# Products with ones in an encoder kernel: split high and low parts in place of float32

## The chip, the core and the metric

The kernel runs on one core of one Trainium2 chip. The core has a matrix engine (TensorE), a vector engine (VectorE), a scalar engine (ScalarE), a general engine (GpSimd), and a queue (SyncE) that starts most transfers. Each engine takes its instructions in order; they wait for one another through semaphores. On-chip memory has 128 partitions. Products are accumulated in eight banks of a memory of their own, 128 x 512 float32 each, which VectorE and ScalarE empty.

The metric is the device time of one execution in microseconds (us), as the median of several runs. A profile is one further execution, in which every instruction was recorded.

## The reference, cut to what matters

One layer of an encoder over a sequence of 1024 positions of width 1024, in float32, and a last norm:

```python
def _rmsnorm(x, w):
    return x * lax.rsqrt(jnp.mean(x * x, axis=-1, keepdims=True) + EPS) * w

h = _rmsnorm(x, attn_norm_w)
proj = h @ w_in                                  # 1024 x 8192
a = glu(first columns); a = dwconv31(a)          # 512 channels
mu = jnp.mean(a, axis=-1, keepdims=True)
var = jnp.mean(jnp.square(a - mu), axis=-1, keepdims=True)
a = silu((a - mu) * lax.rsqrt(var + EPS) * ln_w + ln_b) @ pw_w
b = (two gated scans of 8 heads, one per direction, normed and gated) @ hgrn_o_w
x = x + (sigmoid(g_a) * a + sigmoid(g_b) * b) @ w_out
h2 = _rmsnorm(x, ffn_norm_w)
gate, val = split(h2 @ ffn_w_up)                 # 2 x 2816 columns
x = x + (silu(dwconv3(gate)) * val) @ ffn_w_down
out = _rmsnorm(x, final_norm_w)
```

What matters here are the means: three of them (the first norm, the LayerNorm of the convolution, the norm ahead of the feed-forward part) run over a direction that the kernel keeps on the partitions.

## The kernel before, in words

**Layout and format.** Activations lie transposed: channels on the 128 partitions, positions along the free axis, in pages of 128 x 512 (a half of the sequence). A float32 operand of a large product is split into a high part, rounded to the format `float32r`, which TensorE takes at its full rate, and a low part, the rest (`split`, line 123: a ScalarE copy and a VectorE subtraction). A product is then three products of parts (`mm3`, lines 148 to 150). Where many columns share the activations, two by two blocks are multiplied with seven products in place of eight (`pair_job`, line 282), taken in the order 1, 2, 6, 7, 5, 4, 3. Pages `hx`, `hy` and `h` hold activation parts, `wp` and `wq` weight parts; in a pair job one `wq` page holds the weights of products 7 and 5, one holds those of 4.

**Order.** TensorE runs in program order. The other engines' instructions are put in order by a planner when the program is built: it takes what is ready first by the times that it assumes, and hands out the pages of a tag as they come free. `pin` (line 121) ties an instruction down: it may not be issued ahead of the one that was traced before it on its engine. A pinned instruction can wait for data, and then whatever stands behind it in the queue waits too. An instruction that is not pinned may be planned ahead of pinned ones.

**Streams.** The large products are a stream of pieces (`run_jobs`, line 194; a piece is two steps of three products, six in all). Between pieces runs a tick, which brings forward the split of a later job's weights (`Weights`, line 169) and the chores that are due (`later`, line 158). In the feed-forward part these splits are pinned.

**The norms.** The sum over partitions of a page of squares is taken by four narrow products, the page as weights against a column of ones (line 611); they leave the 512 sums on partitions, as 128 x 4. Root and power run there on GpSimd (`rstd_small`, line 590). To have the factor of each position on every partition, the four columns are written as four diagonals of a 128 x 512 page, and a float32 product of an all-ones matrix with it copies each diagonal over all partitions (`spread`, line 595, the product in line 601). The diagonals are made by four ScalarE operations (line 600), or, for the norm ahead of the feed-forward part, by one pinned GpSimd operation (line 621). The LayerNorm's mean is one float32 product of the all-ones matrix with the sum of four pages (line 1065).

**Where they stand.** The first half of x is normed before it is turned, and uses none of this. `second_norm` (line 752) norms the second half. The LayerNorm loop (line 1056) runs twice, between pieces of the pair jobs. The norms ahead of the feed-forward part (line 1759) run inside its first job: the factor is applied only to the results, so the products start without it. Piece 1 of that job is filled in line 1742; then line 1757 puts off the splits of the `hy` pages for product 4 by four and five ticks (one of them is of `t6`, which line 1726 makes in a page of tag `tm`); two more pieces follow, then the two norms up to their diagonals (line 1761), one piece, the fetches for product 3, seven pieces, and then the two products of line 601 and their copies (line 1766). The weights of products 7 and 5 of that job are split at the tick of its fourth piece, those of product 4 at its seventh.

**Pages.** Tag `tm` has four pages of 128 x 512, which temporary results of all parts share, the diagonals too.

**Stores.** As the residual sum x2 is made (`x2_evac`, line 1581), each of its 16 pages, scaled by the norm's weights, is stored to `d_h2` (line 1599). Line 1764 reads back four of them.

Of the kernel before, what the change touches and what calls it, by code (L numbers as in the profile page):

```python
# [18 lines left out]
P = 128  # L19
# [28 lines left out]
def tile_hybrid_encoder(  # L48
# [51 lines left out]
    def bank(tag):  # L100
        return ps.tile([P, H], F32, tag=tag, name=nm(tag), bufs=BANKS[tag])

    def page(pool, tag, bufs, dt=F32):
        return pool.tile([P, H], dt, tag=tag, name=nm(tag), bufs=bufs)

    def tmp():
        return page(mp, "tm", 4)
# [373 lines left out]
    make_identity(nc, ident)  # L481
    mhalf = cp.tile([P, 1], F32, name="mhalf")
    G.memset(mhalf, -0.5)
    ones_m = cp.tile([P, P], F32, name="ones_m")
    cp.tile([P, ALIGN // 4 - 8], F32, name="offset")
    G.memset(ones_m, 1.0)

# [63 lines left out]
    def scratch(name, *dims):  # L551
        if not dims:
            return dp.tile([P, H], F32, name=name)
        return [scratch(f"{name}_{i}", *dims[1:]) for i in range(dims[0])]
# [12 lines left out]
    d_x0 = dp.tile([P, 4, ND, P], F32, name="d_x0")  # L567
    d_xt = [[d_x0[:, :, k, :], scratch(f"d_xt_{k}")] for k in range(ND)]
    d_x2 = scratch("d_x2", ND, 2)
    d_h2 = scratch("d_h2", ND, 2)  # L570
    d_t4 = scratch("d_t4", ND // 2)
    d_g = scratch("d_g", NF, 2)
    d_us = [dp.tile([P, 4, ND // 2 * P], F32, name=f"d_us_{n}") for n in range(3)]
# [16 lines left out]
    def rstd_small(dst, ss, n, late=False):  # L590
        hold = pin if late else lambda i: i
        hold(G.tensor_scalar(dst, ss, 1.0 / n, EPS, op0=ALU.mult, op1=ALU.add))
        hold(G.tensor_tensor(dst, dst, mhalf.to_broadcast(list(dst.shape)), op=ALU.pow))

    def spread(r, b, rs, diag=None, late=False):

        if diag is None:
            diag = tmp()
            for c in range(4):
                A.activation(diag[:, c * P : (c + 1) * P], ident, AF.Copy, scale=r[:, c : c + 1])  # L600
        T.matmul(b, ones_m, diag, start=True, stop=True)
        do = A.copy(rs, b)
        if late:
            pin(do)
        return rs

    def rstd_over_partitions(sq, n, tag, rs, early=False):

        b = bank(tag)
        for c in range(4):  # L610
            T.matmul(
                b[:, c : c + 1], sq[:, c * P : (c + 1) * P], ones_m[:, 0:1], start=True, stop=True
            )
        r = cp.tile([P, 4], F32, name=nm("r4"), tag="r4", bufs=2)
        V.tensor_copy(r, b[:, 0:4])
        rstd_small(r, r, n, early)
        diag = None
        if early:
            diag = tmp()
            pin(  # L620
                G.tensor_tensor(
                    diag.rearrange("p (c e) -> p c e", c=4),
                    view(ident, 0, [[0, 4], [1, P]]),
                    view(r, 0, [[1, 4], [0, P]]),
                    op=ALU.mult,
                )
            )
        yield
        yield spread(r, bank(tag), rs, diag, early)

    def first_norm():

# [119 lines left out]
    def second_norm():  # L752
        xs, ss = x_in[4:], ss2
        banks = []

        def turn(k):
            b = bank("tr")
            for i in range(4):
                T.transpose(b[:, i * P : (i + 1) * P], xs[i][:, k * P : (k + 1) * P], ident)
            banks.append(b)  # L760

        turn(0)
        yield
        rstd_small(ss, ss, D)
        rs = spread(ss, bank("ob"), page(p0, "rs", 1))
        yield
        for k in range(ND):
            b = banks[k]
            raw, xt = ev(), tmp()
            V.scalar_tensor_tensor(raw, b, vec("attn", k), rs, op0=ALU.mult, op1=ALU.mult)  # L770
            hl = split(hx(), hx(), raw, G)
            A.copy(xt, b)
            if k + 1 < ND:
                turn(k + 1)
            nc.sync.dma_start(d_h[k][1], raw)
            nc.sync.dma_start(d_xt[k][1], xt)
            if k < NK2:
                h12.append(hl)
            else:
                ht[3].append(hl)  # L780
            yield
# [268 lines left out]
    def total(ts, o):  # L1050
        V.tensor_tensor(o, ts[0], ts[1], op=ALU.add)
        for t in ts[2:]:
            V.tensor_tensor(o, o, t, op=ALU.add)
        return o

    for half in range(2):
        xs = []
        for j in range(NCW):
            if j % 2 == 0:
                both = p1.tile([P, 2, H], F32, tag="ca", name=nm("cx"), bufs=2)  # L1060
            nc.sync.dma_start(both[:, j % 2, :], d_cv[j][half])
            xs.append(both[:, j % 2, :])
        s_pairs.fill(LN_FILL)
        mean = bank("ob")
        T.matmul(mean, ones_m, total(xs, tmp()), start=True, stop=True)
        for t in xs:
            V.scalar_tensor_tensor(t, mean, -1.0 / CW, t, op0=ALU.mult, op1=ALU.add)
        s_pairs.fill(LN_FILL)
        sqs = [tmp() for _ in xs]
        for sq, t in zip(sqs, xs):  # L1070
            A.activation(sq, t, AF.Square)
        rstd = rstd_over_partitions(total(sqs, sqs[0]), CW, "ob", tmp())
        next(rstd)
        s_pairs.fill(5)
        rs = next(rstd)
        for j, xn in enumerate(xs):
            V.tensor_tensor(xn, xn, rs, op=ALU.mult)
# [503 lines left out]
    def x2_evac(i):  # L1581


        def evac(half, acc):
            xt = ev()
            to = xt if half else xt.rearrange("p (c t) -> p c t", c=4)
            nc.sync.dma_start(to, d_xt[i][half])
            t = page(p4, "x2", 2)
            V.tensor_tensor(t, acc, xt, op=ALU.add)
            nc.sync.dma_start(d_x2[i][half], t)  # L1590
            if i == 0:
                A.activation(sq_sum[half], t, AF.Square)
            else:
                sq = tmp()
                A.activation(sq, t, AF.Square)
                V.tensor_tensor(sq_sum[half], sq_sum[half], sq, op=ALU.add)
            g = page(p4, "xq", 5)
            A.activation(g, t, AF.Copy, scale=vec("ffn", i))
            nc.sync.dma_start(d_h2[i][half], g)
            x2[i][half] = g  # L1600

        return evac
# [158 lines left out]
        next(st)  # L1761
    s_ffn.fill(1)
    for k in range(NK2):
        late_parts(5 + k // 2, 3, fetch(d_h2[k + NK2][1]))
    s_ffn.fill(7)
    rstd2 = [next(st) for st in stats]

# [301 lines left out]
```

## Time and profile before

| | |
|---|---|
| time, median of 3 runs | 1722.05 us (1721.24 to 1723.18) |
| span of the profiled execution, first to last instruction | 1720.0 us |
| ScalarE, line 600: 12 diagonal pieces | 0.39 us each |
| GpSimd, line 621: 2 diagonal pages | 1.04 and 1.69 us |
| stores of line 1599 | 16 of 256 KB, SyncE 0.33 us each, landed after 3.8 us |
| transfers, all | 308.28 MB, mean 179 GB/s |

The profile gives a span alone, from the first to the last instruction; the runs' times are those of the device. The median of the runs is 2.05 us above the profiled span. In its rows PE is TensorE, ACT is ScalarE, DVE is VectorE, POOL is GpSimd, SP is SyncE. A row names the line of the kernel, the operation, what it writes and reads, and in brackets how long the engine stood idle before it and for whom. Line 124 is the body of `split`, so its rows are told apart by the pages that they write. A TensorE record lasts longer than the distance to the next one, since products overlap; what a product takes of the stream is read from the distance of starts. A float32 product is two records.

### The profile page before, as it was taken

Reading aid. Unit: us, or ns where it says so; the run is one execution under the profiler, and the core shown is the slowest. Engines: PE = TensorE matmul, PEld = TensorE weight load, DVE = VectorE, ACT = ScalarE, POOL = GpSimd, SP = SyncE. Lnnn points to the kernel's source line nnn. Section 1 sums busy time; section 2 is a strip of 40 time slices with the busy share of each in tenths; the row PEclk is TensorE's granted clock in tenths of the full one; section 3 lists DMA queues with packets and bytes.
Section 4 is the critical chain, followed back from the end, with each engine's and each line's share of the span. In section 5 each row is a group of like instructions: output and inputs, shape, how many; then the busy total and the mean of one; then the engine's idle time right before and its main releaser. Section 6 shows DMA issues by size and latency. Waiting matters only on the chain.

```text
span 1720.0 us, 30762 instructions
## 1 busy us (share of the span) xinstructions
PE 1699.1 (99%) x11902; PEld 1416.2 (82%) x11902; DVE 1256.6 (73%) x1937; ACT 825.0 (48%) x1544; POOL 240.7 (14%) x281
## 2 busy tenths in 40 slices
PE   8999999999999999999999999999999999999998
PEld 6878888788788888888888888888888888888787
DVE  4599999745779888888656466667777776657865
ACT  6443443233577777776442245444434433542334
POOL 1212222200001111111100002122222222000110
PEclk9999999999999999999999999999999999999999
DMA  8777888854673444435689466577778776783842
GB/s 281 238 181 177 201 191 189 203 160 148 202 261 91 146 127 133 128 116 200 223 277 279 143 205 199 147 159 153 165 166 174 171 172 154 229 266 102 215 95 99
DMA packets 337096, 308.28 MB, mean 179 GB/s; under 512 B 17582, under 2 KB 249142, under 8 KB 336950
## 3 DMA queue, kind: packets, MB, share of 16 engines
q1 hardware_dynamic: 289590, 267.51, 49.1%
q0 software_dynamic: 47360, 38.81, 15.5%
q8 instruction: 93, 1.52, 0.4%
q14 instruction: 53, 0.43, 0.1%
HBM read 201.40 MB, written 87.03 MB: 168 GB/s over the span
## 4 chain that ended last, share of the span: by engine, by line
PE 61%; DVE 1%; ACT 1%; DMA 0%; issue 0%; POOLq 0%; ACTq 0%; SPq 0%; DVEq 0%
PE mm L148 14%; PE mm L150 14%; PE mm L149 14%; PE sc L148 3%; PE sc L150 3%; PE sc L149 3%; PE ob L1375 2%; PE tr L148 1%; PE tr L150 1%; PE tr L149 1%; PE sc L1197 1%; PE sc L1283 1%; PE mm L1334 1%; PE sc L1334 1%; PE ob L1197 0%
## 5 line engine op out<-in xcount | busy, mean ns | idle before, releaser
L148 PE MATMUL mm<-hx,wp 128*128 128x512 f32 x1068 | 426.9, 400 | 2.3 <-ACT tm L851 1.4
L150 PE MATMUL mm<-hx,wp 128*128 128x512 f32 x1068 | 416.9, 390 | 0.5 <-DVE wp L124 0.5
L149 PE MATMUL mm<-hx,wp 128*128 128x512 f32 x1068 | 416.2, 390 | 0.0
L124 ACT CAST wp<-wr 128x1024 fp32r<-128x1024 f32 (+2 forms) x147 | 147.3, 1003 | 217.8 <-PE mm L149 180.3
L148 PEld LDWEIGHTS mm<-hx,wp 128*128 128x128 f32 x1068 | 200.6, 188 | 45.0 <-DVE ev L800 2.2
L150 PEld LDWEIGHTS mm<-hx,wp 128*128 128x128 f32 x1068 | 200.5, 188 | 44.4 <-DVE wp L124 1.6
L149 PEld LDWEIGHTS mm<-hx,wp 128*128 128x128 f32 x1068 | 200.8, 188 | 39.2 <-issue 0.7
L124 DVE TENSOR_TENSOR wp<-wr,wp 128x1024 fp32r<-128x1024 f32 (+2 forms) x145 | 169.1, 1167 | 39.1 <-ACT wp L124 32.7
L1039 DVE SCALAR_TENSOR_TENSOR acc<-gl,v_b,acc 128x1024 f32<-128x1024 f32 x120 | 148.7, 1272 | 0.4
L440 ACT COPY su<-mm 128x512 f32<-128x512 f32 x82 | 47.7, 582 | 80.1 <-PE mm L150 80.1
L1315 POOL DMA_DIRECT2D S<-D x64 | 36.3, 573 | 284.2 <-ACT S L1313 155.6
L1144 DVE TENSOR_TENSOR qF<-qF,tb 128x512 f32<-128x512 f32 x96 | 65.5, 684 | 13.3 <-ACT A L1178 12.7
L124 ACT CAST wq<-sw 128x1024 fp32r<-128x1024 f32 x41 | 43.2, 1053 | 61.2 <-PE mm L149 32.9
L148 PE MATMUL tr<-hx,wp 128*128 128x512 f32 x180 | 70.5, 392 | 0.0
L150 PE MATMUL tr<-hx,wp 128*128 128x512 f32 x180 | 70.1, 389 | 0.0
L149 PE MATMUL tr<-hx,wp 128*128 128x512 f32 x180 | 70.0, 389 | 0.0
L1144 DVE TENSOR_TENSOR kG<-kG,tb 128x512 f32<-128x512 f32 x96 | 65.5, 685 | 4.7 <-ACT A L1178 2.5
L1652 DVE SCALAR_TENSOR_TENSOR tm<-gp,v_a,tm 128x512 f32<-128x512 f32 x88 | 66.0, 750 | 4.0 <-ACT tm L1650 2.0
L301 POOL DMA_DIRECT2D sw<-in_ffn_w_up_dram x38 | 49.8, 1498 | 116.5 <-DMA sw<-in_ffn_w_up_dram 76.7
L148 PE MATMUL mm<-hy,wp 128*128 128x512 f32 x164 | 64.2, 391 | 0.0
L148 PE MATMUL sc<-hy,wq 128*128 128x512 f32 x164 | 64.2, 391 | 0.0
L150 PE MATMUL sc<-hy,wq 128*128 128x512 f32 x164 | 63.8, 389 | 0.0
(375 smaller groups left out, 3723.3 us busy)
## 6 DMA issues: line engine op xcount, KB each, us to landing
wr<-in_w_in_dram SPq DMA_DIRECT2D x48, 512.0 KB, 5.0
wr<-in_ffn_w_up_dram SPq DMA_DIRECT2D x22, 512.0 KB, 5.1
sw<-in_w_in_dram SPq DMA_DIRECT2D x38, 256.0 KB
d_g<-ft SPq DMA_DIRECT2D x38, 256.0 KB, 2.0
sw<-in_ffn_w_up_dram SPq DMA_DIRECT2D x38, 256.0 KB, 3.5
sw<-in_ffn_w_up_dram POOLq DMA_DIRECT2D x38, 256.0 KB, 6.2
wr<-sw POOLq DMA_DIRECT2D x32, 256.0 KB, 3.3
wr<-wr POOLq DMA_DIRECT2D x32, 256.0 KB, 3.4
```

The lines of the kernel that those rows point to most:

```text
L124: parts = A.copy(hi, src), eng.tensor_tensor(lo, src, hi.bitcast(F32), op=ALU.subtract)
L148: T.matmul(acc, whi[:, k, :], ahi, start=first, stop=False, skip_group_check=again)
L149: T.matmul(acc, whi[:, k, :], alo, start=False, stop=False, skip_group_check=again)
L150: T.matmul(acc, wlo[:, k, :], ahi, start=False, stop=last, skip_group_check=again)
L301: G.dma_start(o, a, accum_op=ALU.add)
L440: A.copy(t, acc)
L1039: V.scalar_tensor_tensor(acc, g[:, k : k + S], tap(k), acc, op0=ALU.mult, op1=ALU.add)
L1144: return V.tensor_tensor(o, a, b, op=op)
L1315: G.dma_start(S_t[g : g + 32, :, g : g + 32], D_t[g : g + 32])
L1334: T.matmul(u[:, sl], kTs[d][:, sl], v[:, c, :], start=True, stop=True)
L1375: T.matmul(o[:, sl], l, r, start=(n == 0), stop=(n == len(terms) - 1))
L1652: V.scalar_tensor_tensor(c, g[:, o + k : o + k + H], vec("fdw", k * NF + j), c, op0=ALU.mult, op1=ALU.add,)
```

## The change

- The all-ones matrix is made as a `float32r` page `ones_r`; `ones_m` is a float32 view of it.
- `diagonals` takes the place of the ScalarE diagonals: the 128 x 4 factors are split into tiny high and low pages, and for each a page of diagonals is made by one VectorE multiplication with the identity. For the norms ahead of the feed-forward part (`early`) the high page stays on GpSimd, and all of these operations are pinned, the split too.
- `all_rows` multiplies the all-ones matrix with the high and the low page, in `float32r`, into the same bank. `spread` uses it, and the LayerNorm's mean, whose sum is split for it.
- In `second_norm` and in the LayerNorm root and diagonals are traced ahead of the pieces that come before the product.
- Of the stores to `d_h2` only the four that are read back are left.

```diff
-    ones_m = cp.tile([P, P], F32, name="ones_m")
+    ones_r = cp.tile([P, P], F32R, name="ones_r")
+    ones_m = ones_r.bitcast(F32)
...
-    d_h2 = scratch("d_h2", ND, 2)
+    d_h2 = scratch("d_h2", ND)
...
-    def spread(r, b, rs, diag=None, late=False):
-
-        if diag is None:
-            diag = tmp()
-            for c in range(4):
-                A.activation(diag[:, c * P : (c + 1) * P], ident, AF.Copy, scale=r[:, c : c + 1])
-        T.matmul(b, ones_m, diag, start=True, stop=True)
-        do = A.copy(rs, b)
+    def diagonals(r, early=False):
+
+        hold = pin if early else lambda i: i
+        tiny = [cp.tile([P, 4], F32R, name=nm("rp"), tag=tag, bufs=2) for tag in ("rh", "rl")]
+        split(*tiny, r, V, early)
+        pages = [page(mp, "tm", 4, F32R) for _ in range(2)]
+        for n, (d, t) in enumerate(zip(pages, tiny)):
+            eng = G if early and n == 0 else V
+            hold(
+                eng.tensor_tensor(
+                    d.rearrange("p (c e) -> p c e", c=4),
+                    view(ident, 0, [[0, 4], [1, P]]),
+                    view(t.bitcast(F32), 0, [[1, 4], [0, P]]),
+                    op=ALU.mult,
+                )
+            )
+        return pages
+
+    def all_rows(b, parts):
+        for n, part in enumerate(parts):
+            T.matmul(b, ones_r, part, start=n == 0, stop=n == len(parts) - 1)
+        return b
+
+    def spread(b, rs, diags, late=False):
+        do = A.copy(rs, all_rows(b, diags))
...
         rstd_small(r, r, n, early)
-        diag = None
-        if early:
-            diag = tmp()
-            pin(
-                G.tensor_tensor(
...
-                )
-            )
+        diags = diagonals(r, early)
         yield
-        yield spread(r, bank(tag), rs, diag, early)
+        yield spread(bank(tag), rs, diags, early)
...
         turn(0)
+        rstd_small(ss, ss, D)
+        diags = diagonals(ss)
         yield
-        rstd_small(ss, ss, D)
-        rs = spread(ss, bank("ob"), page(p0, "rs", 1))
+        rs = spread(bank("ob"), page(p0, "rs", 1), diags)
...
-        mean = bank("ob")
-        T.matmul(mean, ones_m, total(xs, tmp()), start=True, stop=True)
+        sums = [page(mp, "tm", 4, F32R) for _ in range(2)]
+        mean = all_rows(bank("ob"), split(*sums, total(xs, tmp()), V))
...
-            nc.sync.dma_start(d_h2[i][half], g)
+            if i >= NK2 and half:
+                nc.sync.dma_start(d_h2[i], g)
...
-        late_parts(5 + k // 2, 3, fetch(d_h2[k + NK2][1]))
+        late_parts(5 + k // 2, 3, fetch(d_h2[k + NK2]))
```

More of the change, by code (lines that the diff above doesn't have):

```diff
@@ L616, in rstd_over_partitions @@
         rstd_small(r, r, n, early)
-        diag = None
-        if early:
-            diag = tmp()
-            pin(
[L621 to L625, printed above, removed]
-                )
-            )
+        diags = diagonals(r, early)
         yield
-        yield spread(r, bank(tag), rs, diag, early)
+        yield spread(bank(tag), rs, diags, early)
     def first_norm():
```

## The prediction

> **What bounds the kernel now.** I read the page first: the busy shares, then the chain of work that ended last.
>
> ```profile
> span 1720.0 us, 30762 instructions
> ...
> PE 1699.1 (99%) x11902; PEld 1416.2 (82%) x11902; DVE 1256.6 (73%) x1937; ACT 825.0 (48%) x1544; POOL 240.7 (14%) x281
> ...
> PE 61%; DVE 1%; ACT 1%; DMA 0%; issue 0%; POOLq 0%; ACTq 0%; SPq 0%; DVEq 0%
> ```
>
> TensorE is busy for 99% of the span and holds nearly all of the chain that is attributed. So a product that gets cheaper shortens the kernel by its own price, an operation on another engine costs nothing while TensorE has its operands in time, and whatever makes TensorE wait is paid in full, since no idle time follows that could take it back. TensorE's order is written out by hand: a late operand stops everything behind it.
>
> Next the timeline of TensorE around one of the edited products (columns: start, duration, engine, line, operation), and the views of lines 601 and 1065.
>
> ```profile
> 422.51 0.40 PE L150 MATMUL mm<-hx,wp 128*128 128x512 f32 x1
> 422.74 1.02 PE L601 MATMUL ob<-tm,ones_m 128*128 128x512 f32 x2
> 423.20 0.80 PE L148 MATMUL mm<-hx,wp 128*128 128x512 f32 x1
> 423.84 0.40 PE L149 MATMUL mm<-hx,wp 128*128 128x512 f32 x1
> ...
> 426.11 0.39 PE L150 MATMUL mm<-hx,wp 128*128 128x512 f32 x1
> ```
> ```profile
> L601 PE MATMUL ob<-tm,ones_m x8: 590/592/595, 39.7 to 1073.6; 128*128 128x512 f32 x8
> ...
> L601 PE MATMUL sc<-tm,ones_m x2: 590/592/595, 1072.3 to 1072.7; 128*128 128x512 f32 x2
> ```
> ```profile
> L1065 PE MATMUL ob<-tm,ones_m x4: 590/592/595, 405.9 to 449.6; 128*128 128x512 f32 x4
> ```
>
> The starts of a steady stream lie 0.227 us apart (423.84 to 426.11 is ten products). From 422.51 to 423.84 there are two such steps, 0.454, and the float32 product: 1.33 - 0.454 = 0.876 us. Each float32 product is two records, so there are 5 of line 601 and 2 of line 1065, seven in all.
>
> **The change part by part.** *Seven products* of 0.876 us become seven pairs of full-rate products, 2 x 0.227 = 0.454 each: 0.42 us saved, seven times, **-2.9 us**. This lies on the path. The 16 narrow float32 products of line 611 stay.
>
> *The dropped stores* (12 of 16 of line 1599) were issued by SyncE beside TensorE's work; no wait of TensorE in that stage names a transfer: 0. If they slow the loads beside them, the gain is below what the waits show, so also 0.
>
> *Norms one and two* (the second half of x, and the LayerNorm twice). ScalarE loses four diagonal pieces each time; VectorE gains a tiny subtraction and two 512-wide multiplications, and each mean gains a ScalarE cast and a VectorE subtraction ahead of its product. The tightest of these is the second LayerNorm mean:
>
> ```profile
> 444.79 0.69 DVE L1053 TENSOR_TENSOR tm<-tm,cx 128x512 f32<-128x512 f32 x1
> ...
> 446.96 1.22 DVE L124 TENSOR_TENSOR wp<-wr,wp 128x1024 fp32r<-128x1024 f32 x1
> ...
> 449.44 0.69 DVE L800 TENSOR_TENSOR ev<-tr,su 128x512 f32<-128x512 f32 x1 [1.26 <-issue]
> ```
> ```profile
> 449.19 1.02 PE L1065 MATMUL ob<-tm,ones_m 128*128 128x512 f32 x2
> ```
>
> The sum is there at 445.48, the product starts at 449.19: 3.7 us of cover. A cast (0.62) and a subtraction (0.69) take 1.3; behind the subtraction already queued (to 448.18) the low part is there at 448.9. Hidden, so 0; should VectorE take the 0.69 and another 1.22 first, it costs about 2.
>
> *The two norms ahead of the feed-forward part* are where a wait is added. These are the rows of the kernel before: ScalarE, VectorE, GpSimd, then TensorE.
>
> ```profile
> 1060.84 0.58 ACT L440 COPY su<-mm 128x512 f32<-128x512 f32 x1
> 1061.32 1.05 ACT L124 CAST wq<-sw 128x1024 fp32r<-128x1024 f32 x1
> 1064.03 1.32 ACT L124 CAST hy<-ft 128x512 fp32r<-128x512 f32 x2 [1.66 <-DMA ft<-d_t]
> ...
> 1066.15 0.62 ACT L124 CAST hy<-ft 128x512 fp32r<-128x512 f32 x1
> ...
> 1067.20 0.62 ACT L124 CAST hy<-tm 128x512 fp32r<-128x512 f32 x1
> ```
> ```profile
> 1061.48 0.15 DVE L615 COPY r<-ob 128x4 f32<-128x4 f32 x1
> 1063.00 0.69 DVE L1680 TENSOR_TENSOR gp<-tr,su 128x512 f32<-128x512 f32 x1 [1.37 <-PE tr L150]
> 1063.61 1.38 DVE L124 TENSOR_TENSOR wq<-sw,wq 128x1024 fp32r<-128x1024 f32 x1
> 1064.91 1.28 DVE L124 TENSOR_TENSOR hy<-ft,hy 128x512 fp32r<-128x512 f32 x2
> ...
> 1068.05 0.68 DVE L124 TENSOR_TENSOR hy<-tm,hy 128x512 fp32r<-128x512 f32 x1
> ```
> ```profile
> 416.30 0.20 POOL L592 TENSOR_SCALAR r<-r 128x4 f32<-128x4 f32 x1 [59.11 <-DVE r L615]
> 416.58 1.03 POOL L593 TENSOR_TENSOR r<-r,mhalf 128x4 f32<-128x4 f32 x1
> ```
> ```profile
> 1062.62 1.29 POOL L1726 TENSOR_TENSOR tm<-tm,xq 128x512 f32<-128x512 f32 x1
> ...
> 1064.11 0.93 POOL L592 TENSOR_SCALAR r<-r 128x4 f32<-128x4 f32 x1
> 1065.13 1.33 POOL L593 TENSOR_TENSOR r<-r,mhalf 128x4 f32<-128x4 f32 x1
> 1066.54 1.04 POOL L621 TENSOR_TENSOR tm<-ident,r 128x512 f32<-128x512 f32 x1
> ...
> 1069.68 1.69 POOL L621 TENSOR_TENSOR tm<-ident,r 128x512 f32<-128x512 f32 x1
> ```
> ```profile
> 1065.47 0.39 PE L148 MATMUL sc<-h,wq 128*128 128x512 f32 x1
> 1065.70 0.39 PE L149 MATMUL sc<-h,wq 128*128 128x512 f32 x1
> 1065.92 0.39 PE L150 MATMUL sc<-h,wq 128*128 128x512 f32 x1
> ```
>
> Before, the norms put nothing but free copies on ScalarE and VectorE here; the whole chain of root and diagonal is GpSimd's, and it has until 1072. Now `split(*tiny, r, V, early)` puts a tiny ScalarE copy and a tiny VectorE subtraction into it for each norm, and `pin` ties them, and the low diagonals, into program order. A pinned instruction may not be issued ahead of the one traced before it on its engine. Counting the steps of the stream: the two norms are traced behind the third piece of the first feed-forward job, and the cast of `wq` (weights of products 7 and 5, 1061.32) at the tick of the fourth piece, pinned too. So that cast, which now runs while GpSimd works, **must stand behind both tiny copies**, and the second copy needs GpSimd's second root. Behind the cast stand the pinned `hy` casts, and on VectorE the low part of `wq` stands behind the second low diagonal. TensorE wants the high part of `wq` at 1065.47 and the low one at 1065.92.
>
> The chain, in the clock of before. GpSimd starts its first scale at 1064.11; VectorE is now idle beside it, so 0.20 and 1.03 as at 416: root at 65.4. Tiny copy: no row shows one on ScalarE; between VectorE's 0.15 and the 0.62 of a 512-wide cast, 0.2, near the copy of the same size: 65.65. First high diagonal on GpSimd 1.04 to 66.75; VectorE's low one waits its turn and holds GpSimd's next scale to 67.4 (the 0.93 at 1064.11 ends with VectorE's 1.38 at 1063.61: the two take turns). Root 68.5, second tiny copy 68.7, cast of `wq` to 69.75.
>
> Then the page that the second low diagonal needs. Tag tm has four pages. `t6` holds one until its `hy` cast and subtraction are done (rows hy<-tm); the first norm's two diagonals hold two until their products, which stand behind products 7 and 5; the second high diagonal, ready first, takes the last. So the second low diagonal waits for `t6`: the `hy` casts follow the `wq` cast, each some 0.53 behind the last, the fourth ends at 71.9, its subtraction (0.68) at 72.6. Those VectorE subtractions are pinned behind line 1680, not behind the diagonal, so nothing closes a circle. Low diagonal 0.69 to 73.35, low `wq` 1.22 to 74.6. TensorE's product of 65.92 starts at 74.6: **+8.7 us**. From below: if GpSimd's diagonal is the one that waits for `t6`, VectorE's goes at 68.9, low `wq` is done near 71: +5.1, and 4.7 with every step at its shortest. From above: two other subtractions (0.68 and 1.22) ahead of the diagonal: +10.6.
>
> *The clock.* TensorE then stands nearly still for 4 us, does two products, and stands again.
>
> ```profile
> 1712.00:1712.50 0.50, 0.16 (x2) 1.00 0.00 0
> ...
> 1714.50:1715.00 0.50, 0.00 (x0) 0.50 0.00 0
> ```
> ```profile
> 13.67 6.39 PE L894 MATMUL mm<-hx,wp 128*128 128x512 f32 x18
> ...
> 20.69 1.63 PE L894 MATMUL mm<-hx,wp 128*128 128x512 f32 x6
> ```
>
> At the end of the kernel the granted clock is halved some two us behind the last work. At the start, 18 products took 6.39 us, where at 0.227 a step and 0.39 for the last it would be 4.25: 2.1 lost to a slow start, part of it waits for operands. I take 1.7 for the return from such a stop, bounds 0 and 2.1. [...]
>
> **Sum**: -2.9 + 8.7 + 1.7 = +7.5. The profiled span of 1720.0 becomes 1727.5; the median of the runs is 2.05 above that span, and I carry this over: **1729.5**.
>
> **The rivals.**
> *The other page* (GpSimd's second diagonal waits for `t6`): -2.9 + 5.1 + 1.7 = +3.9, 1725.9; without the clock's part 1724.2. For it: only which of two instructions gets the last page. Against: VectorE's needs one step more (0.15) before it can start.
> *Cheaper products and no wait*, on the other side: if the cast and subtraction of `wq` stay done by 1065.47 and 1065.92, only -2.9 is left, 1719.1, within 0.2%. It is decided there: the second tiny copy would have to be done by 1064.2, 4.5 us sooner than I make it. For it: the ScalarE row at 1061.32 shows how early the cast can go when nothing holds it. Against: the pin, and GpSimd's 1062.62 row, behind which the roots start.
> *One more wait*: the LayerNorm mean's low part late as above, or the longer VectorE queue: +2 to +3 on the forecast, 1732. *Not what it says*: a full-rate product might cost what a float32 one does; then the seven pairs save nothing, and 2.9 more joins the forecast, 1732.4; against it stand the 0.227 steps of the same format.
>
> **How the numbers follow.** Forecast 0.58, other page 0.22, no wait 0.10, one more wait or no saving 0.10. About 0.2% (3.4 us) is what a measurement of this kernel can tell from no change. Slower: forecast and last rival, 0.68, and nearly half of the other page: 0.78. Same: the rest of the other page and most of the no-wait case, 0.19. Faster: 0.03, if small shifts elsewhere add to the saving. The range leaves out the no-wait case and the far end: 1723.5 (other page, short steps, no clock loss) to 1733.0 (+10.6 and 2.1: 1731.9, and a us of shifts).
>
> **What would show it.** Right: full-rate records on the edited lines, adding 0.454 to the stream; the cast wq<-sw behind two tiny copies near 1068.7; TensorE idle before its first sc<-h,wq, again at the third, which waits for VectorE; the second low diagonal behind hy<-tm; a clock below 1 for some us. Wrong: the cast at 1061 as before, or a tiny copy ready by 1064. The forecast falls if the roots start earlier, or if a later wait of TensorE shrinks by what this one adds.

## The result, and the profile after

The changed kernel takes 1732.78 us (median of 5 runs, 1732.18 to 1733.41). The kernel before takes 1723.17 (median of 5 runs, the three of the table above among them). The ratio is 1.0061, with a 95% interval of 1.0049 to 1.0074: slower by 8 to 13 us. The page of the kernel after:

```profile
span 1730.8 us, 30738 instructions
...
PE 1699.8 (98%) x11902; PEld 1416.6 (82%) x11902; DVE 1263.4 (73%) x1952; ACT 824.3 (48%) x1539; POOL 238.9 (14%) x281
```

The span grew by 10.8 us, TensorE's busy time by 0.7. So in sum the growth is time in which TensorE stands: in its busy time, products that last longer (below) and products that became cheaper about cancel. The view of the waits says for whom (waiting engine, what it writes and its line, whom it waited for, sum, times, longest):

```profile
PE sc L148 <- ACT wq L124: 4.0, 1, 4.0
PE sc L150 <- DVE wq L124: 4.0, 1, 4.0
PE mm L148 <- DVE ev L809: 2.6, 3, 1.3
```
```profile
PE mm L148 <- DVE ev L800: 0.7, 1, 0.7
```

The first two are new. The third stood at 0.7 before the change (the second view, of the kernel before, where the line was 800). The timelines of ScalarE, VectorE and TensorE show the first two in the making.

```profile
1065.52 0.19 ACT L124 CAST rp<-r 128x4 fp32r<-128x4 f32 x1 [4.01 <-POOL r L594]
1068.56 0.19 ACT L124 CAST rp<-r 128x4 fp32r<-128x4 f32 x1 [2.85 <-POOL r L594]
1068.66 1.04 ACT L124 CAST wq<-sw 128x1024 fp32r<-128x1024 f32 x1
...
1071.65 0.62 ACT L124 CAST hy<-tm 128x512 fp32r<-128x512 f32 x1
```
```profile
1072.39 0.68 DVE L124 TENSOR_TENSOR hy<-tm,hy 128x512 fp32r<-128x512 f32 x1
1073.11 0.69 DVE L605 TENSOR_TENSOR tm<-ident,rp 128x512 fp32r<-128x512 f32 x1
1073.72 1.22 DVE L124 TENSOR_TENSOR wq<-sw,wq 128x1024 fp32r<-128x1024 f32 x1
```
```profile
1065.33 0.39 PE L150 MATMUL mm<-hx,wp 128*128 128x512 f32 x1
1069.76 0.79 PE L148 MATMUL sc<-h,wq 128*128 128x512 f32 x1 [4.04 <-ACT wq L124]
1070.35 0.63 PE L149 MATMUL sc<-h,wq 128*128 128x512 f32 x1
1074.99 0.79 PE L150 MATMUL sc<-h,wq 128*128 128x512 f32 x1 [4.01 <-DVE wq L124]
1075.58 0.63 PE L148 MATMUL sc<-h,wq 128*128 128x512 f32 x1
1076.01 0.63 PE L149 MATMUL sc<-h,wq 128*128 128x512 f32 x1
...
1079.85 0.42 PE L149 MATMUL mm<-hx,wq 128*128 128x512 f32 x1
1080.11 0.39 PE L150 MATMUL mm<-hx,wq 128*128 128x512 f32 x1
```

ScalarE does two casts of 0.19 us, and in front of each it stands, 4.01 and 2.85 us, for GpSimd's root. The cast of the page `wq`, begun at 1061.32 before, comes behind them at 1068.66. On VectorE the second low diagonal waits for its page until `t6` is split (hy<-tm at 1072.39), and the low part of `wq` comes behind it. TensorE's third product starts at 1074.99, in place of 1065.92. Then its starts lie 0.43 us apart (1075.58 to 1076.01) where 0.227 is usual, until 1079.85. The granted clock by stretches (from and to; busy us and instructions of PE, PEld, DVE, ACT, POOL; clock; DMA share; GB/s):

```profile
1066.00:1070.00 4.00, 0.24 (x1) 0.24 (x2) 1.54 (x2) 1.44 (x3) 3.40 (x4) 0.95 0.40 153
1070.00:1080.00 10.00, 5.99 (x14) 4.20 (x15) 6.15 (x8) 4.08 (x8) 0.00 (x0) 0.51 0.40 117
1080.00:1085.00 5.00, 5.00 (x24) 4.05 (x23) 3.11 (x5) 2.88 (x7) 0.00 (x0) 1.00 0.10 29
```

For ten microseconds TensorE has half its clock.

**A ledger.** TensorE runs the same large products in the same order in both kernels, so the start of one product, after minus before, says how much has been lost up to there. Ahead of the feed-forward part, at 1059.6 us, it is +0.1. Each of the five other cheaper products shows its 0.4 us at its place, but waits have taken all of it back by then. The three waits for line 809, up to 343 us, take 1.8 us more than the waits at the same products before (0.70 and 0.09 us there), and one at 859 us takes 0.5 more (0.77 after, 0.24 before). Another -0.8 in that +0.1 is no work of the change: at 30 us, ahead of every edited product, the kernel after already stands at -0.8, since the clock rises to full at 14.92 us in its trace and at 17.72 in the trace before. At the third late product the ledger is +9.1; at the last one at half clock +11.4; behind the two cheaper feed-forward products +10.7; at the end +10.7. So the large loss stands in the feed-forward part, and behind 1085 us nothing is added and nothing taken back.

### The profile page after: what moved, and what is told of

The parts are those of the page before. It is cut to its first block, busy times and chain, and to the rows that moved or that the text cites. A ratio compares the mean times of both kernels' runs of the same rounds, so it can differ in the third digit from the quotient of the medians.

```text
span 1730.8 us, 30738 instructions
## 1 busy us (share of the span) xinstructions
PE 1699.8 (98%) x11902; PEld 1416.6 (82%) x11902; DVE 1263.4 (73%) x1952; ACT 824.3 (48%) x1539; POOL 238.9 (14%) x281
## 3 DMA queue, kind: packets, MB, share of 16 engines
q8 instruction: 93, 1.52, 0.4%
## 4 chain that ended last, share of the span: by engine, by line
PE 37%; issue 12%; DMA 1%; DVE 1%; ACT 0%; POOL 0%; SPq 0%; POOLq 0%; ACTq 0%; DVEq 0%
PE mm L150 8%; PE mm L148 8%; PE mm L149 8%; PE sc L150 3%; PE sc L148 3%; PE sc L149 3%; PE tr L149 1%; PE tr L148 1%; PE tr L150 1%; PE ob L1384 0%; DMA tm<-d_g 0%; DMA d_a<-ev 0%; DMA tm<-d_gc 0%; PE sc L1922 0%; DMA A<-d_bm 0%
```

## The experiments

Each run's ratio is to the kernel before, run on the same chip, with its 95% interval. I call "ledger" the comparison of starts just described.

**1. The feed-forward norms alone, undone and done.** Undone in the changed kernel:

```diff
-        diags = diagonals(r, early)
-        yield
-        yield spread(bank(tag), rs, diags, early)
+        if early:
+            diag = tmp()
+            pin(
+                G.tensor_tensor(
+                    diag.rearrange("p (c e) -> p c e", c=4),
+                    view(ident, 0, [[0, 4], [1, P]]),
+                    view(r, 0, [[1, 4], [0, P]]),
+                    op=ALU.mult,
+                )
+            )
+            yield
+            b = bank(tag)
+            T.matmul(b, ones_m, diag, start=True, stop=True)
+            pin(A.copy(rs, b))
+            yield rs
+            return
+        diags = diagonals(r)
+        yield
+        yield spread(bank(tag), rs, diags)
```

> The changed kernel, with the two norms of the FFN stage alone as they were before: one float32 diagonal by GpSimd, one float32 product each. Theory: the whole loss arises there. TensorE's first product after the FFN norms ran 10.6 us later than before, counted from the products just ahead of the stage, and nothing was added behind it, so the time falls by 10.6, to about 1722.2 us, level with the kernel before (ratio 0.999 to 1.001); the two waits of 4.0 us on the pages wq are gone, and the products behind them run at the full clock again. Rival: a good part of the loss is spread (the longer wait for the layer norm's mean, 0.9 us, a lower clock all over, later transfers): then it stays at 1725 us or above.

Measured: 1721.51 us, ratio 0.9997 (0.9988 to 1.0006). The loss is gone, and both waits on `wq` with it.

The other way round, the same edit alone put into the kernel before (`split` of the 128x4 factors, GpSimd's high and VectorE's low diagonal, two full-rate products, for the two feed-forward norms only):

> The kernel before, with the edit of the two FFN norms alone: the rest is as before. Theory: the edit of these two norms makes the whole difference and the other five cheaper products give nothing at the end, so 1723.2 + 10.6 = 1733.8 us (ratio 1.006). Rival: the five other products' saving of 5 x 0.42 = 2.1 us is contained in the changed kernel's time, which would then be 1734.9 us or more here; a second rival, that the loss needs the other edits too, gives less than 1731 us.

Measured: 1733.67 us, ratio 1.0066 (1.0051 to 1.0081), with the same two waits of 4.0 us. Both sides agree: this one place makes the loss. The interval of the first run leaves the worth of the five other products open between -2.1 and +1.0 us.

**2. What holds the page.** Two edits, each in a kernel of its own, that move one step of the order: in the first this one split isn't pinned, in the second `t6` comes from another ring of pages.

```diff
-                w[7], w[5] = both(col, pool)
+                w[7], w[5] = both(col, pool, late and not now)
...
-        t7, t6, t5 = tmp(), tmp(), tmp()
         last = k == NK2 - 1
+        t7, t6, t5 = tmp(), ev() if last else tmp(), tmp()
```

> The changed kernel; only the place of one split moves: the w7/w5 page of the FFN's first job isn't held behind the norms' instructions any more, so ScalarE can cast it between the norms' two tiny copies and VectorE makes its low part ahead of the second diagonal. Nothing else is changed. Theory: the stall is the order of instructions on ScalarE and VectorE, so it shrinks by what the page comes earlier: low part done at about 70 us in place of 75 (1000 us left out), the third product about 4 us late in place of 9, a time of 1726 to 1728 us. Rival: what holds the page is not the place in the order (its operands, or a buffer that comes free late): no change, 1732.8 us.

> The changed kernel; one of the three temporaries of the last pair in the FFN's stage ahead takes a page of another ring, so that the second norm's diagonals don't wait for it. Theory: VectorE's second diagonal no longer sits ahead of the page's low part until its page is free, the low part ends at about 71.3 us (1000 left out) in place of 75, and the stall falls by 3.4 to 3.9 us: about 1729 us, with both waits on wq shorter and the first of them unchanged in its cause (ScalarE's tiny copies). Rival: the diagonal waits for the root of the second norm and not for its page: no change, 1732.8 us.

Measured: 1729.21 us, ratio 1.0044 (1.0027 to 1.0061), for the first, and 1728.91, 1.0041 (1.0027 to 1.0054), for the second. The intervals touch that of the changed kernel, so the rows have to carry the reading: in both kernels the waits moved as the order of instructions did, and both rivals fall. TensorE's rows, the split that isn't pinned first:

```profile
1065.26 0.50 PE L148 MATMUL sc<-h,wq 128*128 128x512 f32 x1 [0.99 <-ACT wq L124]
...
1069.56 0.79 PE L150 MATMUL sc<-h,wq 128*128 128x512 f32 x1 [3.56 <-DVE wq L124]
```
```profile
1074.70 0.79 PE L148 MATMUL sc<-h,wq 128*128 128x512 f32 x1 [4.08 <-ACT wq L124]
...
1076.55 0.80 PE L150 MATMUL sc<-h,wq 128*128 128x512 f32 x1 [0.64 <-DVE wq L124]
```

Where only the page of `t6` is changed, the first wait stays (4.08) and the second shrinks from 4.01 to 0.64: the two waits have two causes, ScalarE's small casts and the page. Where the split is free, the cast comes between the two small ones and the first wait shrinks to 0.99. By its median it fell 1 to 3 us short of its expectation (in its trace the third product is 4.9 us late, 4 were expected): the low part, planned behind the second tiny subtraction, took 2.08 us in place of 1.22 while GpSimd made a diagonal, and the clock stayed low for as long as with the other edit (starts 0.43 us apart from 1070.15 to 1073.99 here, from 1077.14 to 1080.98 there).

**3. The clock.** The waits are filled with products that nobody reads, 17 ahead of the first product with `wq` and 17 ahead of the third:

```diff
+                def busy():
+                    for _ in range(idle):
+                        pin(T.matmul(b, ones_r, acts(1)[0][0], start=True, stop=True))
...
+                busy()
...
+                busy()
...
+            idle=17 if n == 0 else 0,
```

> The changed kernel, with 17 products more ahead of each of TensorE's two waits of 4.0 us in the FFN's first job: full-rate products of the ones with a page that is there, into a bank that nobody reads, 17 x 0.227 = 3.86 us each time, so they fit into the waits. Theory: a part of the loss isn't the waits but the lower clock that the standing TensorE brought (products 0.427 us apart in place of 0.227 for some 4.9 us after them). With TensorE kept at work the clock stays, the products behind come 0.227 us apart at once, and although it computes more the time falls by 2.4 to 2.6 us, to about 1730.3; the waits that are left are 0.1 to 0.3 us each. Rival: the slow steps come from the late operands themselves: the time stays at 1732.8 us or rises.

Measured: 1730.38 us, ratio 1.0046 (1.0030 to 1.0061): 2.4 us less than the changed kernel by the medians, with 34 products more. By the intervals that difference can be off by some 3 us; the traces are sharper. TensorE's timeline, and the clock of the same stretch as above:

```profile
1069.94 4.13 PE L455 MATMUL ob<-hx,ones_r 128*128 128x512 f32 x17
1074.59 0.50 PE L463 MATMUL sc<-h,wq 128*128 128x512 f32 x1 [0.53 <-DVE wq L124]
1074.93 0.39 PE L148 MATMUL sc<-h,wq 128*128 128x512 f32 x1
1075.16 0.39 PE L149 MATMUL sc<-h,wq 128*128 128x512 f32 x1
```
```profile
1070.00:1080.00 10.00, 9.47 (x42) 7.42 (x41) 7.67 (x11) 6.02 (x11) 0.00 (x0) 1.00 0.42 124
```

The third product is as late as in the changed kernel (0.5 us of wait is left), but the clock is 1.00 in place of 0.51, and the starts behind it lie 0.23 us apart at once. Against the kernel before, the ledger of this run goes from +8.7 at the third product to +8.8 behind the stretch, where that of the changed kernel goes from +9.1 to +11.5. So about 2.4 us of the loss is the clock, and the rest of what the feed-forward part loses is the wait.

**4. The layer norm's mean.** In the changed kernel VectorE makes the low part of the sum. Its timeline before, then after, then ScalarE's after, then TensorE's before and after:

```profile
340.54 0.69 DVE L1053 TENSOR_TENSOR tm<-tm,cx 128x512 f32<-128x512 f32 x1 [0.31 <-DMA cx<-d_cv]
341.15 0.68 DVE L800 TENSOR_TENSOR ev<-su,mm 128x512 f32<-128x512 f32 x1
```
```profile
340.26 0.69 DVE L1062 TENSOR_TENSOR tm<-tm,cx 128x512 f32<-128x512 f32 x1 [0.23 <-DMA cx<-d_cv]
341.69 0.69 DVE L124 TENSOR_TENSOR tm<-tm,tm 128x512 fp32r<-128x512 f32 x1 [0.74 <-ACT tm L124]
342.31 0.68 DVE L809 TENSOR_TENSOR ev<-su,mm 128x512 f32<-128x512 f32 x1
```
```profile
341.04 0.62 ACT L124 CAST tm<-tm 128x512 fp32r<-128x512 f32 x1 [3.70 <-DVE tm L1062]
```
```profile
341.88 0.50 PE L148 MATMUL mm<-hx,wp 128*128 128x512 f32 x1
```
```profile
343.04 0.50 PE L148 MATMUL mm<-hx,wp 128*128 128x512 f32 x1 [0.93 <-DVE ev L809]
```

Before, the eviction `ev` came directly behind the sum. Now VectorE stands 0.74 us for ScalarE's cast, subtracts, and only then evicts; TensorE waits 0.93 us for the bank (0.09 before). The mean's product itself comes at 407 us: nothing is in a hurry but what stands behind the subtraction. The edit is one word, the engine of the low part, on top of run 1's first kernel:

```diff
-        mean = all_rows(bank("ob"), split(*sums, total(xs, tmp()), V))
+        mean = all_rows(bank("ob"), split(*sums, total(xs, tmp()), G))
```

> The kernel with the FFN norms as before, and the low part of the layer norm's mean taken from VectorE's queue to GpSimd's. Theory: the change's second loss is at the first of the two means: VectorE stands there behind ScalarE's cast (0.74 us in the changed kernel's trace), and the eviction behind it keeps TensorE waiting at 343 us for 0.9 to 1.3 us in the kernels with the split mean against 0.1 and 0.3 in the two traces without it. With the low part on GpSimd that wait falls to about 0.3 us, and the time by some 0.7 us against the kernel with the FFN norms as before: a ratio to the kernel before of 0.999 to 1.000. Rival: the wait there has another cause (the transfers cx that VectorE's sums wait for): it stays at 0.9 us or more, and the time stays too.

Measured: 1721.30 us, ratio 0.9992 (0.9983 to 1.0001). That time can't be told from run 1's; the trace can (VectorE, GpSimd, TensorE):

```profile
338.52 1.42 DVE L1078 TENSOR_TENSOR tm<-tm,cx 128x512 f32<-128x512 f32 x2 [5.99 <-DMA cx<-d_cv]
339.86 0.68 DVE L825 TENSOR_TENSOR ev<-su,mm 128x512 f32<-128x512 f32 x1
```
```profile
340.79 1.29 POOL L124 TENSOR_TENSOR tm<-tm,tm 128x512 fp32r<-128x512 f32 x1 [1.91 <-issue]
```
```profile
341.13 0.39 PE L148 MATMUL mm<-hx,wp 128*128 128x512 f32 x1
```

The eviction follows the sum again, and TensorE doesn't wait. In the ten traces with the mean's low part on VectorE the wait at this product is 0.5 to 2.3 us (0.93 after, 1.08 in run 1's first kernel); in the two without a split mean it is 0.09 and 0.33, and in the two with the low part on GpSimd (this run and the last one below) there is none. How much of it arrives at the end of the kernel the times can't tell.

**5. What TensorE's time is worth early on.** I took it that the second norm's saving is lost since VectorE and the transfers set the end of the convolution stage. Extra products, on top of run 1's first kernel, turn the sign round (`for _ in range(extra): T.matmul(b, ones_r, parts[0], start=True, stop=True)` ahead of the pair):

> The kernel with the FFN norms as before, and 8 full-rate products more (8 x 0.227 = 1.8 us) directly ahead of the second norm's product, into the same bank. It asks what TensorE's time is worth at that place. Theory: nothing or little: the convolution stage behind it ends when VectorE and its transfers are through, TensorE's first product past the last wait there stands at 341.6 to 343.0 us in all the traces but one, with the cheaper product and without, and the waits in between (1.3 and 1.1 us) shrink by what TensorE comes later. So that product stays within 0.7 us of its place, and the time within 0.5 us of the same kernel without the 8. Rival: the time is counted in full: +1.8 us at that product and at the end.

> The kernel with the FFN norms as before, and 4 full-rate products more (0.91 us) ahead of each of the layer norm's four means, into the same bank: 3.6 us in all, twice what the change saved there with each sign turned. Theory: behind the convolution stage TensorE sets the end, so it is counted in full: +3.6 us at the end. Rival: these places too have waits that give the time back, above all the one at the end of the stage of the heads at 859 us, so that less than half of it arrives: +1.8 us or less.

> As the run with 8 products more ahead of the second norm's product, with 4 (0.9 us). In that run 1.9 us were inserted at 39 us, 0.7 of them were left at 343, as expected; but then 3.3 us came on top, the first 1.4 at 521 us, where TensorE stands for 1.3 us and the profile shows nothing that it waits for, though the order of its instructions is the same. Theory: what is inserted there is absorbed by 343 us (0 to 0.4 us left), and the standing at 521 hangs on how many instructions lie ahead; then the time is either level with the kernel without extra products, within 0.5 us, or shows the gap of 1.3 us again at 521 and is up by 1.3 to 3.5 us. Rival: the late stage costs follow from TensorE being late at 39 us, in proportion: half of the 4.0 us, +2.0, with no gap at 521.

Measured: 8 products more at the second norm (1.8 us): 1726.07 us, ratio 1.0025 (1.0016 to 1.0034), which is 4.8 us over the same kernel without them. 4 products more there (0.9 us): 1723.70, 1.0008 (0.9999 to 1.0018), 1.9 over. 4 products more ahead of each mean: 1723.42, 1.0008 (0.9999 to 1.0017), 1.9 over. (The differences are those of the ratios; by their intervals each can be off by about 2 us.) For this last run the expectation counted wrongly: the layer norm has two means, not four (the other two of its four products are the root's, without extra products here), so 1.8 us were put in and 1.9 came out. By the time alone that could be chance; the ledger against run 1's kernel agrees, from -0.7 at 400 us to +1.3 behind the second mean. So what TensorE does there is counted in full, and the rival falls.

At the second norm the theory fell. At 343 us the ledger shows 0.7 of the 1.9 us, as expected; but then other waits came. With 8 products TensorE stood at 521 us, with nothing shown that it waits for, though the instructions of all engines stand in the same order but for the 8 products:

```profile
523.22 0.50 PE L148 MATMUL mm<-hx,wp 128*128 128x512 f32 x1 [1.31 <-issue]
```

With 4 this gap is not there; the wait at 343 us is 2.13 us instead, and the clock halves behind it (0.56 in the mean from 344.0 to 347.5 us). In that trace the ledger stands at +0.6 at 310 us and at +3.2 behind the slow stretch. I can't settle what makes the 3 us that come on top of what was put in. What the run with 8 does show is that TensorE's time at 39 us isn't free.

**6. A better version.** If only the places of the small instructions are wrong, the split products can be kept. First everything of the feed-forward norms on GpSimd, four small instructions and four diagonals, with `t6` in the other ring:

```diff
+        if early:
+            hi, lo = tiny
+            pin(G.tensor_copy(hi, r))
+            pin(G.tensor_tensor(lo, r, hi.bitcast(F32), op=ALU.subtract))
...
-            eng = G if early and n == 0 else V
+            eng = G if early else V
```

> The changed kernel, with the FFN norms' four small instructions (two casts, two low parts) and all four diagonals on GpSimd, one behind the other, and one temporary of the last pair in another ring as in the run before, so that ScalarE and VectorE meet nothing of the norms ahead of the page wq. The products stay split and full-rate. Theory: the loss is only where the small instructions stand; GpSimd's chain of 0.2 + 1.0 + 2 x 0.3 + 2 x 1.0 us per norm ends at about 72.6 us (1000 left out), just ahead of the products that read it (73.2 in the kernel before), so both waits on wq are gone and the two products' saving of 0.83 us is kept: 1732.8 - 11.5 = 1721.3 us, ratio 0.998 to 1.0005. Rival: GpSimd's longer chain ends late and TensorE waits for the second norm's diagonals: 1722 to 1725 us.

Measured: 1727.44 us, ratio 1.0029 (1.0020 to 1.0039). The rival came true, and worse. Its waits, and GpSimd's last rows:

```profile
PE ob L621 <- POOL tm L610: 3.1, 2, 2.1
```
```profile
1071.83 1.88 POOL L594 TENSOR_TENSOR r<-r,mhalf 128x4 f32<-128x4 f32 x1
...
1074.64 2.93 POOL L610 TENSOR_TENSOR tm<-ident,rp 128x512 fp32r<-128x512 f32 x2
```

The waits on `wq` are gone, but a root that took 1.01 us beside an idle VectorE takes 1.88 here, two diagonals 2.93. The chain ends at 77.6, TensorE stands 3.1 us, and its clock halves once more (starts 0.43 us apart from 1078.22 to 1083.34). So the chain was shortened: both halves' sums in one 128x8 tile, one scaling, one root, one cast, one low part, then the four diagonals:

```diff
+        r = cp.tile([P, 8], F32, name="r8")
...
+            V.tensor_copy(r[:, 4 * h : 4 * h + 4], b[:, 0:4])
+        rstd_small(r, r, n, True)
+        pin(G.tensor_copy(hi, r))
+        pin(G.tensor_tensor(lo, r, hi.bitcast(F32), op=ALU.subtract))
...
+        for h in range(2):
+            for t in (hi, lo):
+                d = page(mp, "tm", 4, F32R)
+                pin(
+                    G.tensor_tensor(
+                        d.rearrange("p (c e) -> p c e", c=4),
+                        view(ident, 0, [[0, 4], [1, P]]),
+                        view(t.bitcast(F32), 4 * h, [[1, 4], [0, P]]),
+                        op=ALU.mult,
+                    )
+                )
...
```

> The changed kernel with another arrangement of the FFN norms: the sums of both halves stand in one 128x8 tile, so GpSimd does one scaling, one root, one cast and one low part for both (some 0.9 + 1.3 + 0.2 + 0.7 us by the run with everything on GpSimd) and then the four diagonals (4 x 1.25); nothing of the norms is on ScalarE or VectorE; the one temporary takes a page of the other ring. Theory: the loss was only where the small instructions stood and, in the run with everything on GpSimd, the length of its chain. From 1065.3 the chain now ends at about 73.4 in place of 77.6, level with the products that read it (73.4), so TensorE waits 0.5 us at most and keeps its clock, and the two products' saving of 0.8 us stays: 0 to 0.8 us under the kernel with the FFN norms as before, which is a ratio to the kernel before of 0.999 to 1.000. Rival: VectorE's two-operand work stretches GpSimd's further; then TensorE waits for the last diagonal by more than 1 us and the ratio is 1.001 or more.

Measured: 1721.22 us, ratio 0.9995 (0.9986 to 1.0004). GpSimd and TensorE:

```profile
1065.89 1.97 POOL L594 TENSOR_TENSOR r<-r,mhalf 128x8 f32<-128x8 f32 x1
...
1072.41 2.02 POOL L658 TENSOR_TENSOR tm<-ident,r8l 128x512 fp32r<-128x512 f32 x1
```
```profile
1074.48 0.50 PE L616 MATMUL ob<-tm,ones_r 128*128 128x512 f32 x1 [0.62 <-POOL tm L658]
```

One wait of 0.62 us is left. It takes back what the two products save: the ledger stands at +0.7 us ahead of the stage and at +0.8 behind it. Then this and the mean's low part on GpSimd together:

> Both of these together: the split products everywhere, both FFN norms in one chain on GpSimd, the mean's low part on GpSimd. Theory: nothing of the change's cost is left, and of its saving the two FFN products (0.8 us) and the four products of the layer norm that stand behind the convolution stage or at its end (4 x 0.42 = 1.7 us) arrive: 1.5 to 2.5 us under the kernel before, a ratio of 0.9985 to 0.9992. Rival: the end is set by transfers elsewhere, and the time stays level with the kernel before, 0.9995 to 1.0005, or rises where one of the two moves failed.

Measured: 1720.04 us (11 runs, 1718.99 to 1720.78), ratio 0.9987 (0.9978 to 0.9996). It is the only version whose interval lies wholly below the kernel before, by 2.2 us (0.7 to 3.8). Since the two feed-forward products about pay for their wait here, this agrees with what the five others should bring, 5 x 0.42 = 2.1 us, once nothing stands still for them.

## Where the prediction held, and which of its steps failed

The direction and the main cause were right, and the total was too small by 2 to 3 us. The steps that failed are terms of the sum: "Hidden, so 0" for the LayerNorm's means, where TensorE's wait grew by 0.8 us; "This lies on the path" for the whole -2.9, of which the five products ahead of the feed-forward part had brought nothing by 1059.6 us; and "I take 1.7" for the clock, which cost 2.4.

*The wait at `wq`: right, by the mechanism that was named.* The tiny casts came at 1065.52 and 1068.56 (forecast 1065.45 and 1068.5), the cast of `wq` ended at 1069.70 (1069.75), the second low diagonal stood behind hy<-tm, and the third product started at 1074.99 (1074.6). The forecast of +8.7 is +9.0 in the ledger; the rest fits a copy of 0.58 us that ScalarE does between the casts of `hy`, at 1070.65, and that the prediction left out. Run 2 shows both links of the chain, the order on ScalarE and the page of `t6`, and the rivals "the other page" and "no wait" fell. (Run 2's second kernel is in effect the case of the other page: its third product came 5.6 us late where 5.1 was forecast.)

*The LayerNorm: wrong.* "Hidden, so 0" looked at when the mean's product needs its operands, and at the second mean. The product had its cover (65 us at the first one). The cost came from what is queued behind the subtraction on VectorE: 0.74 us of standing there, and TensorE waits 0.8 us more at 343 us. Run 4 shows it by moving only the subtraction to another engine: the wait is gone.

*The savings: right at their places, wrong as a sum.* In the ledger the layer norm's four products, the second norm's, and the two of the feed-forward part each give their 0.4 us. But "since no idle time follows that could take it back" failed for the five early ones: forecast are -2.1 us ahead of the feed-forward part, and the ledger has +0.1. Run 1 leaves these five and all that goes with them at -0.5 us (-2.1 to +1.0). Of the waits that took the saving back, the 0.8 us at 343 is the mean's subtraction; the others, at 283, 303 and 859 us, change from trace to trace by up to a microsecond, with the split mean and without it, and no run shows that the change makes them longer. With the mean's low part on GpSimd, the last run has its 2.2 us.

*The clock: right in kind, too small.* I took 1.7 us, with an upper bound of 2.1 from the start of the kernel. No run shows the 1.7; in its place the ledger shows 2.4 (from +9.1 to +11.5), and in run 3, where the clock stays, 0.1. The half clock lasted 10.2 us, from 1069.64, 0.1 us before the first stop ended, to 1079.88, with the second stop in it. TensorE worked slowly for 4.9 us behind the second, eleven steps that were 0.2 us longer each: these are the 2.4 us.

*The last rival.* Its sum is wrong, though it did not come true: if a full-rate product cost the 0.876 us of a float32 one, a pair would cost twice that, and the seven pairs would lose 6.1 us in place of saving nothing.

*The dropped stores and norm one (second half of x)*: no wait in any trace points to them. They weren't tried alone.

*The sum.* By the ledger, whose two traces lie 10.7 us apart, the terms are +0.1 ahead of the feed-forward part (forecast -2.1; without the later rise of the clock in the trace before it would be +0.9), +9.0 for the wait (8.7), +2.4 for the clock (1.7) and -0.8 for the two products there (-0.8). At least two thirds of what the forecast of +7.5 lacks thus lie ahead of the feed-forward part. The medians of the runs lie 9.6 us apart; the difference of a microsecond between the two figures is within what single executions of one kernel differ by.

## What to carry to other kernels

An instruction of 0.2 us that is tied into the order of a busy engine delays everything queued behind it by what it waits for: ask of each small instruction in a chain between engines not only when its result is needed, but what stands behind it. In this kernel the long chain did best on an engine with nothing urgent behind it, whole and with as few steps as possible. And where TensorE stands for some two microseconds or more, allow for a loss of its clock besides the wait: here stops of 1.93 to 4.08 us were followed by half the clock, though one of 2.33 us was not. Count it from the last stop, behind which the 4.9 us of slow work came here.

## What the runs showed of the hardware

**Stops and the clock.** Behind the waits of 4.0 us in the changed kernel the half clock lasted 10.2 us; where the split isn't pinned (stops of 0.99 and 3.56 us) the mean of 0.62 from 1065 to 1074 us makes 6.8. Shorter stops brought it too: stops of 1.93, 1.97 and 2.13 us (ending at 325, 97 and 344 us of three traces). Behind the first, with the page of `t6` changed, the mean clock is 0.52 from 326.5 to 330.0 us; behind the second, with one chain on GpSimd, 0.53 from 97.2 to 100.7 and 0.99 up to 104.0; behind the third, with 4 extra products at the second norm, 0.56 from 344.0 to 347.5 and 0.96 up to 351.0. In each of the three that makes some 3.4 us at half clock in these stretches. A stop of 2.33 us, with everything on GpSimd, brought none, and neither did one of 1.52 us at 322 us of that trace, behind which the starts lie 0.23 us apart. The stretches behind the stops of 2.13 and of 2.33 us; the clock is the third figure from the end:

```profile
344.00:347.50 3.50, 3.50 (x9) 2.75 (x10) 2.22 (x3) 0.03 (x1) 0.00 (x0) 0.56 0.51 162
```
```profile
344.00:347.50 3.50, 3.50 (x15) 2.90 (x16) 2.25 (x3) 0.71 (x2) 0.00 (x0) 1.00 0.47 147
```

So the length of a stop alone doesn't decide it (1.93 us brought it, 2.33 did not), and what does isn't shown. A spell of 3.4 us costs some 1.4 to 1.6 us, an estimate from the rows (9 products in such a stretch in place of 15 or 16, 0.227 us apart). The mean clock goes with the time of single executions of one kernel, which differ by several microseconds: of the nine of the kernel with everything on GpSimd, the slowest (1730.34 us) has the lowest, 0.995, and the fastest (1723.95) the highest, 0.999.

**VectorE and GpSimd.** Beside VectorE's operations of two operands GpSimd's instructions took up to twice as long: a root 1.01 us in the changed kernel, where VectorE was idle, and 1.88 with everything on GpSimd, a diagonal 1.04 at 1068.84 in the changed kernel and 1.69 at 1069.68 in the kernel before. So did VectorE's low part of `wq`, 1.22 us in the changed kernel and 2.08 where the split isn't pinned: it began at 1067.42 there, and GpSimd's diagonal ran until 1068.42, so a microsecond went by beside the diagonal, and then about its usual time. GpSimd's scaling of 0.20 us (1064.19 in the changed kernel) took 0.52 at 1066.92, and 0.93 and 0.52 at 1064.11 and 1067.66 of the kernel before; each of the three ended 0.05 to 0.07 us behind an operation of VectorE that had begun earlier. So work moved to GpSimd is to be priced by what VectorE does at the time.
